# A hybrid attention trunk on one core: two groups of transposes one step later, the second row block's w2 sums in other PSUM banks, the first evacuations in another order

## The chip, the cores and the metric

One core of a Trainium2 chip runs the whole program. The time is device microseconds (us), the median of three runs: 1257.64 us (1256.57 to 1257.86). A difference of about 0.2%, 2.5 us, is what such a measurement can tell from no change.

## What is computed

Two layers, each of a half-step SwiGLU feed-forward, a mixer of three parallel branches, and a second half-step feed-forward, on 256 tokens of width 1024. Cut to what matters here:

```
x = x + 0.5 * (silu(n(x) @ w1) * (n(x) @ w3)) @ w2          # d_ff = 2816
h = n(x);  z = h @ W_in                                     # queries, keys, values, gates of all branches
y_na  = neighbourhood attention;  y_gla = gated linear attention;  y_mla = latent attention
mixed = sig(g0) * (y_na @ w_br_na) + sig(g1) * (y_gla @ w_br_gla) + sig(g2) * (y_mla @ w_br_mla)
x = x + mixed @ w_out
x = x + 0.5 * (second SwiGLU)
```

## The kernel before

All products are made from pairs of fp32r numbers: a high half and the rest, a low half, and three matmuls (high by high, high by low, low by high) for one fp32 product. The weights come as **units** of 128 x 2048 numbers over the SP queue into three raw buffers. ScalarE (ACT) copies the high half (L142), VectorE (DVE) subtracts it from the raw numbers to give the low half (L148), each in two pieces of 128 x 1024. The two L148 of a unit are called a *pair* below. Four buffers hold split units.

Nothing is scheduled by a tool: each engine takes its instructions in the order in which the program is written. Side work stands in small generators (tasks). After each piece of matmuls the program calls `tick()`: it first issues splits for the units ahead (`fill`), and then advances each waiting task whose count has run down. `spawn(gen, n)` sets the first count, `yield n` the next. So one count more puts a task's next step behind one more piece of 12 matmuls (of 128 x 512), and on every engine behind what else that tick issues.

PSUM has eight banks, in two groups of four: `acc` (sums) and `ta` (transposes and attention). A new tile takes the bank of its group that has been free for longest, and its first writer waits for the last reader of that bank.

The places that the change touches:

- **`wide_out`** makes the sums with w2 (11 units) or w_out (4 units) for the row blocks t = 0 and 1, two banks each. For all units but the last two it goes unit by unit, t = 0 and then t = 1, 12 matmuls each; the last two units are held and done at the end, output half by output half. In the feed-forward it follows `fform`, whose 20 chunks (i = 2 to 21) each take two `acc` banks; DVE's L481 is the last to read them.
- **`ffn` at the start of the program** evacuates three chunks at once (`fdrain`): chunks 0 (in `ta` banks) and 1 (in `acc` banks) come ready made from `start_first`, chunk 2 from the first `fform`. An evacuation of chunk 2 starts with two ACT copies (L480), which DVE's L481 waits for.
- **`na_tr`** transposes the queries of neighbourhood attention (L695, spawned at L1122 with a count of 3).
- **`gla_chain`**, linear attention: the last step scales its output on DVE (eight L1103, 128 x 128 each), and after `yield 1` eight transposes (L695) on TensorE (PE), and the high half (ACT L246) and low half (DVE L247) of the result.
- **`branch`** multiplies each branch's output with its weights, in the order na, mla, gla; four pieces of 12 matmuls each (output half h, row block t). They are called na1 to na4, mla1 to mla4 and gla1 to gla4. DVE multiplies each sum by its gate (L1184 for mla and gla). The add into `mixed` (L1186) is done by GpSimd (POOL) for mla and by DVE for gla.
- **`mix_task`**, spawned in each gla piece (L1188) with a count of 2: four PE transposes (L1195) of a finished block of `mixed`, high half on ACT (L246), low half on DVE (L247). The four tasks are called T1 to T4, in the order of gla1 to gla4. T1 and T2 hold output half 0 for t = 0 and 1. The first unit of w_out reads T1 for t = 0 and T2 for t = 1. In each piece of `wide_out` the first four matmuls read the high half, and the fifth is the first to read the low half.

Of the kernel before, what the change touches and what calls it, by code (L numbers as in the profile page):

```python
# [45 lines left out]
def body(tc, T):  # L46
# [3 lines left out]
    with ctx:  # L50
# [146 lines left out]
        def spawn(gen, wait=1):  # L197
            tk = Task(gen, wait)
            tasks.append(tk)
            return tk  # L200
# [181 lines left out]
        def run(g):  # L382
            return spawn(g)
# [30 lines left out]
                    tick()  # L414
            return tks

        def wide_out(first, lhs, nu, done):
            accs = {}
            hold = []
            for u in range(nu):  # L420
                hl = unit()
                if u >= nu - 2:
                    hold.append((u, hl))
                    continue
                for t in range(2):
                    if u == 0:
                        accs[t] = (acc_t(), acc_t())
                    wide_burst(accs[t], lhs, u, hl, t, u == 0, False)
                    tick()
            for t in range(2):  # L430
                for h in range(2):
                    for u, hl in hold:
                        for kk in range(2):
                            a = kk * 1024 + h * 512
                            mm(accs[t][h], lhs(0, u, kk, t), hl[:, 0, a:a + 512], False, False)
                            mm(accs[t][h], lhs(0, u, kk, t), hl[:, 1, a:a + 512], False, False)
                            mm(accs[t][h], lhs(1, u, kk, t), hl[:, 0, a:a + 512], False, u == nu - 1 and kk == 1)
                    done(t, h, accs[t][h])
                    tick(True)
# [12 lines left out]
        def ffn(norms, after, prefetch, first=None, out=None):  # L452
# [42 lines left out]
            def fform(i):  # L495
                hl = unit()
                acc = [(at_t() if first is not None and i == 3 else acc_t()) for _ in range(2)]
                for b in range(2):
                    o = acc[b].rearrange("p (w t n) -> p w t n", w=2, t=2)
                    for k in range(8):  # L500
                        a = k * 256 + b * 128
                        both = xT[:, :, :, k, :].rearrange("p t w n -> p w t n")
                        mm(o, hl[:, 0, a:a + 128], both, k == 0, False)
                        mm(o[:, 0], hl[:, 1, a:a + 128], xT[:, :, 0, k, :], False, k == 7)
                    if b == 0:
                        tick()
                if i == (FIRST_R if first is not None else 2):
                    rs_bcast()
                    if first is not None:
                        for j in range(2):  # L510
                            drains[j] = run(fdrain(j, first[j][0][:, :256], first[j][1][:, :256]))
                        for j, a in held:
                            drains[j] = run(fdrain(j, a))
                if "x" in rs_b:
                    drains[i] = run(fdrain(i, acc))
                else:
                    held.append((i, acc))
                tick()

            us, drains, held = {}, {}, []  # L520
# [33 lines left out]
                if out is None:  # L554
                    after(t, h)

            wide_out(True, lhs, NCH, done)


        def mixer(l, norms, after, prefetch):  # L560
# [444 lines left out]
            def gla_chain(deps):  # L1005
# [94 lines left out]
                for t in range(2):  # L1100
                    for h in range(4):
                        sl = slice(h * 128, h * 128 + 128)
                        DVE.scalar_tensor_tensor(out=gy[t][:, sl], in0=gy[t][:, sl], scalar=rr[t][:, h:h + 1],  # L1103
                                                 in1=sg[t][:, sl], op0=ALU.mult, op1=ALU.mult)
                yield 1
                for j in range(2):
                    ps = four(gy, j * 256)
                    ysplit(ps, "gla", j)
# [10 lines left out]
            u_tk = []  # L1119
            dense8(512, ev_v, between=up_proj(0, 384, ev_uq, u_tk))  # L1120
            nq = dense8(512, ev_nqk("q"))
            q_tk = spawn(na_tr("q", nq), 3)  # L1122
            dense8(512, ev_copy(gvt), between=up_proj(1, 512, ev_ukv, u_tk))
            mla_tk = spawn(mla_chain(u_tk), 1)
            gl_tk = spawn(gla_gates(), 1)
# [42 lines left out]
            def branch(i, key):  # L1168
                lh = lambda hl, k, t: yT[key, k // 2][hl][:, (k % 2) * 256 + t * 128:(k % 2) * 256 + t * 128 + 128]
                for h in range(2):  # L1170
                    hl = unit()
                    for t in range(2):
                        acc = acc_t()
                        burst(acc, lh, hl, range(4), t, 512, True, True)
                        if i < 2:
                            g = gates[:, t, i * 1024 + h * 512:i * 1024 + h * 512 + 512]
                        else:
                            g = late.pop((h, t))
                        if i == 0:
                            m = mixed[h, t] = s2()  # L1180
                            DVE.tensor_tensor(out=m, in0=acc, in1=g, op=ALU.mult)  # L1181
                        else:
                            m = mixed[h, t]
                            DVE.tensor_tensor(out=g, in0=acc, in1=g, op=ALU.mult)  # L1184
                            e = DVE if i == 2 else POOL
                            e.tensor_tensor(out=m, in0=m, in1=g, op=ALU.add)  # L1186
                        if i == 2:
                            mt[h, t] = spawn(mix_task(h, t), 2)  # L1188
                        tick()

            def mix_task(h, t):
# [19 lines left out]
            def done(t, h, acc):  # L1211
                sl = slice(h * 512, h * 512 + 512)
                DVE.tensor_tensor(out=x[:, t, sl], in0=acc, in1=x[:, t, sl], op=ALU.add)
                after(t, h)
            wide_out(True, lhs, 4, done)


        def spawner(ap, into, params_of=None):
# [146 lines left out]
```

## Time and profile before

| | |
|---|---|
| median of three runs | 1257.64 us (1256.57, 1257.64, 1257.86) |
| the profiled execution's own time | 1256.21 us |
| its span, first to last instruction | 1254.4 us |
| PE busy (matmul / weight load) | 1237.7 us (99%) / 1058.5 us (84%) |
| DVE / ACT / POOL busy | 894.8 (71%) / 710.4 (57%) / 219.4 us (17%) |
| DMA | 228.58 MB, mean 182 GB/s |
| chain that ended last | PE 93%, DVE 4%, ACT 1%, DMA 1%, issue 1% |

A view by time gives an instruction's start, its length, engine, line, what it writes and reads, a count where equal ones follow each other, and in brackets how long the engine stood idle before it and what ended that. Ends of matmuls are modelled and overlap the next start by some 0.16 us, so gaps on PE are read from the idle time in brackets or from starts.

### The profile page before, as it was taken

How to read it: one execution, taken by the hardware profiler on the slowest of the kernel's cores; microseconds unless marked ns; L12 is line 12 of the kernel's file. 1: busy time of each engine (PE TensorE's matmuls, PEld its weight loads, DVE VectorE, ACT ScalarE, POOL GpSimd, SP SyncE). 2: the span in 40 equal slices, each digit the busy share in tenths (PEclk: the TensorE clock that was granted, in tenths of full speed). 3: DMA queues.
4: the chain of work that ended last, by engine and by line, in shares of the span. 5: the costliest groups of instructions: out<-in, count | busy, mean ns of one | idle time of the engine just before them, and what ended most of it. 6: DMA issues, size and time to landing. Idle time of an engine off the chain costs nothing.

```text
span 1254.4 us, 18062 instructions
## 1 busy us (share of the span) xinstructions
PE 1237.7 (99%) x6996; PEld 1058.5 (84%) x6996; DVE 894.8 (71%) x1382; ACT 710.4 (57%) x1303; POOL 219.4 (17%) x167
## 2 busy tenths in 40 slices
PE   7999999999999999999999999999999999999998
PEld 7888888889987888888888888888899878888887
DVE  5888736679755868887378886375896577788862
ACT  6556535657665465655366555355686644665541
POOL 0222101132011112221012220021322020122200
PEclk9999999999999999999999999999999999999999
DMA  8655644562543544556345556347526434555560
GB/s 304 214 185 201 234 169 160 175 222 93 197 171 132 198 172 170 200 181 248 142 171 222 184 185 241 128 162 246 175 91 208 166 134 171 199 201 174 196 235 34
DMA packets 37942, 228.58 MB, mean 182 GB/s; under 512 B 5776, under 2 KB 6928, under 8 KB 13280
## 3 DMA queue, kind: packets, MB, share of 16 engines
q1 hardware_dynamic: 37680, 227.36, 51.1%
q8 instruction: 55, 0.90, 0.3%
q14 instruction: 31, 0.25, 0.1%
q0 software_dynamic: 32, 0.07, 0.0%
q10 hardware_dynamic: 144, 0.00, 0.0%
HBM read 224.26 MB, written 1.05 MB: 180 GB/s over the span
## 4 chain that ended last, share of the span: by engine, by line
PE 93%; DVE 4%; ACT 1%; DMA 1%; issue 1%; POOL 0%; DVEq 0%; SPq 0%; ACTq 0%
PE acc L372 86%; PE ta L372 4%; DVE hl L148 2%; PE ta L695 1%; DMA raw<-in_l_f_w 1%; PE ta L263 1%; ACT junk L1095 0%; POOL sm L573 0%; PE ta L782 0%; ACT hl L142 0%; PE ta L1195 0%; PE ta L680 0%; DVE s L489 0%; DVE s L1181 0%; DVE s L1103 0%
## 5 line engine op out<-in xcount | busy, mean ns | idle before, releaser
L148 DVE TENSOR_TENSOR hl<-raw,hl 128x1024 fp32r<-128x1024 f32 (+2 forms) x422 | 568.1, 1386 | 95.4 <-ACT hl L142 84.5
L142 ACT ACTIVATE hl<-raw 128x1024 fp32r<-128x1024 f32 (+2 forms) x422 | 417.1, 1040 | 103.8 <-PE acc L372 89.9
L372 PE MATMUL acc<-xT,hl 128*128 128x512 f32 (+1 forms) x2768 | 472.8, 332 | 0.9 <-DVE s L481 0.5
L372 PEld LDWEIGHTS acc<-xT,hl 128*128 128x128 f32 x2768 | 413.6, 188 | 57.8 <-DVE s L481 0.8
L372 PE MATMUL acc<-hl,xT 128*128 128x512 f32 (+1 forms) x1584 | 361.8, 383 | 0.0
L372 PEld LDWEIGHTS acc<-hl,xT 128*128 128x128 f32 x1584 | 291.8, 188 | 46.9 <-issue 1.7
L372 PE MATMUL acc<-hl,s 128*128 128x512 f32 x1344 | 312.3, 392 | 0.9 <-DVE s L481 0.9
L372 PEld LDWEIGHTS acc<-hl,s 128*128 128x128 f32 x1344 | 252.0, 189 | 54.2 <-DVE s L481 1.3
L482 POOL TENSOR_TENSOR s<-s,rsb 128x512 f32<-128x512 f32 x80 | 111.9, 1399 | 355.8 <-DVE s L481 355.8
L491 ACT ACTIVATE s<-s 128x256 fp32r<-128x256 f32 x82 | 34.2, 418 | 172.5 <-DVE s L489 172.5
L481 DVE TENSOR_TENSOR s<-acc,s 128x256 f32<-128x256 f32 x158 | 59.7, 419 | 58.5 <-ACT s L480 58.5
L573 POOL TENSOR_TENSOR sm<-sm,mhalf 128x4 f32<-128x4 f32 (+2 forms) x24 | 35.8, 1493 | 200.4 <-DVE sm L577 198.9
L284 POOL TENSOR_TENSOR sm<-sm,mhalf 128x1 f32<-128x1 f32 x12 | 14.1, 1176 | 295.1 <-DVE sm L283 295.1
L480 ACT ACTIVATE s<-acc 128x256 f32<-128x256 f32 x158 | 50.6, 371 | 0.0
L266 ACT ACTIVATE xT<-ta,gain 128x128 fp32r<-128x128 f32 x80 | 22.8, 368 | 35.6 <-PE ta L263 35.6
L247 DVE TENSOR_TENSOR s<-ta,s 128x512 fp32r<-128x512 f32 (+1 forms) x46 | 26.7, 604 | 22.6 <-ACT s L246 22.3
L246 ACT ACTIVATE s<-ta 128x512 fp32r<-128x512 f32 (+1 forms) x46 | 23.0, 531 | 34.4 <-PE ta L695 14.7
L487 ACT ACTIVATE s<-s 128x256 f32<-128x256 f32 x82 | 34.2, 419 | 11.2 <-POOL s L482 0.8
L550 DVE SCALAR_TENSOR_TENSOR x<-acc,x 128x512 f32<-128x512 f32 (+1 forms) x20 | 11.3, 580 | 39.7 <-PE acc L372 39.7
L372 PEld LDWEIGHTS ta<-s,s 64*64 64x64 f32 (+3 forms) x720 | 30.6, 145 | 7.0 <-issue 5.9
L372 PE MATMUL ta<-s,s 64*64 64x128 f32 (+4 forms) x720 | 35.9, 260 | 0.0
L493 DVE TENSOR_TENSOR s<-s,s 128x256 fp32r<-128x256 f32 x82 | 34.0, 416 | 1.9 <-ACT s L491 1.9
(161 smaller groups left out, 643.9 us busy)
## 6 DMA issues: line engine op xcount, KB each, us to landing
raw<-in_l_f_w SPq DMA_DIRECT2D x124, 1024.0 KB, 4.8
raw<-in_l_in_g SPq DMA_DIRECT2D x16, 816.0 KB, 4.4
raw<-in_l_in_late SPq DMA_DIRECT2D x8, 1024.0 KB, 4.9
raw<-in_l_out SPq DMA_DIRECT2D x8, 1024.0 KB, 4.8
raw<-in_l_f_up SPq DMA_DIRECT2D x6, 1024.0 KB, 4.8
raw<-in_l_in_m SPq DMA_DIRECT2D x4, 1024.0 KB, 4.7
raw<-in_l_in_gr SPq DMA_DIRECT2D x4, 1024.0 KB, 4.9
raw<-in_l_in_r SPq DMA_DIRECT2D x4, 1024.0 KB, 4.8
```

The costliest lines, as they stand in the source:

```text
L142: ACT.activation(out=hls[j][:, 0, sl], in_=raws[j][:, sl], func=AF.Copy)
L148: DVE.tensor_tensor(out=hl[:, 1, sl], in0=r[:, sl], in1=hl[:, 0, sl].bitcast(F32), op=ALU.subtract)
L246: ACT.activation(out=hi, in_=ps, func=AF.Copy)
L247: DVE.tensor_tensor(out=lo, in0=ps, in1=hi.bitcast(F32), op=ALU.subtract)
L372: PE.matmul(out=out, lhsT=lhsT, rhs=rhs, start=start, stop=stop, skip_group_check=True)
L480: ACT.activation(out=g[:, j, :], in_=a[j][:, 256:], func=AF.Copy)
L481: DVE.tensor_tensor(out=g[:, j, :], in0=a[j][:, :256], in1=g[:, j, :], op=ALU.add)
L482: POOL.tensor_tensor(out=g, in0=g, in1=rb[:, None, :].to_broadcast([128, 2, 256]), op=ALU.mult)
L487: ACT.activation(out=g[:, 0, :], in_=g[:, 0, :], func=AF.Silu)
L491: ACT.activation(out=o[:, 0, :], in_=g[:, 0, :], func=AF.Copy)
L493: DVE.tensor_tensor(out=o[:, 1, :], in0=g[:, 0, :], in1=o[:, 0, :].bitcast(F32), op=ALU.subtract)
L573: POOL.tensor_tensor(out=r[:, :n], in0=ss[:, :n], in1=mhalf[:, :n], op=ALU.pow)
```

## The change

Five edits:

1. `wide_out` is told from which group the banks of t = 1 come: `ta` in the feed-forwards, `acc` as before for w_out.
2. The first evacuations go 1, 2, 0 where they went 0, 1, 2.
3. `gla_chain` yields 2 where it yielded 1 between the scaling and the transposes.
4. The task with the transposed queries is spawned with 4 where it was 3.
5. `mix_task` is spawned with 3 where it was 2.

```diff
-        def wide_out(first, lhs, nu, done):
+        def wide_out(bank1, lhs, nu, done):
...
                     if u == 0:
-                        accs[t] = (acc_t(), acc_t())
+                        accs[t] = (bank1(), bank1()) if t else (acc_t(), acc_t())
...
                     if first is not None:
-                        for j in range(2):
-                            drains[j] = run(fdrain(j, first[j][0][:, :256], first[j][1][:, :256]))
+                        drains[1] = run(fdrain(1, first[1][0][:, :256], first[1][1][:, :256]))
                         for j, a in held:
                             drains[j] = run(fdrain(j, a))
                 if "x" in rs_b:
                     drains[i] = run(fdrain(i, acc))
                 else:
                     held.append((i, acc))
+                if first is not None and i == FIRST_R:
+                    drains[0] = run(fdrain(0, first[0][0][:, :256], first[0][1][:, :256]))
                 tick()
...
-            wide_out(True, lhs, NCH, done)
+            wide_out(at_t, lhs, NCH, done)
...
-                yield 1
+                yield 2
                 for j in range(2):
                     ps = four(gy, j * 256)
                     ysplit(ps, "gla", j)
...
-            q_tk = spawn(na_tr("q", nq), 3)
+            q_tk = spawn(na_tr("q", nq), 4)
...
-                            mt[h, t] = spawn(mix_task(h, t), 2)
+                            mt[h, t] = spawn(mix_task(h, t), 3)
...
-            wide_out(True, lhs, 4, done)
+            wide_out(acc_t, lhs, 4, done)
```

No instruction is added or taken away. Lines of the changed kernel are one higher from L510 on.

DVE in layer 0, from the last scaling of linear attention on (s_3847 and s_3856 are high halves of that branch's transposed output). Before:

```order
L1103 SCALAR_TENSOR_TENSOR s_3702<-s_3702,sm,s_1955 128x128 x4
L1184 TENSOR_TENSOR gates<-acc,gates 128x512
L247 TENSOR_TENSOR s_3848<-ta,s_3847 128x512
L247 TENSOR_TENSOR s_3857<-ta,s_3856 128x512
L1184 TENSOR_TENSOR gates<-acc,gates 128x512
L148 TENSOR_TENSOR hl<-raw,hl 128x1024 x2
L1184 TENSOR_TENSOR gates<-acc,gates 128x512 x2
L148 TENSOR_TENSOR hl<-raw,hl 128x1024 x2
```

The same place on DVE now:

```order
L1104 SCALAR_TENSOR_TENSOR s_3702<-s_3702,sm,s_1955 128x128 x4
L1185 TENSOR_TENSOR gates<-acc,gates 128x512 x2
L148 TENSOR_TENSOR hl<-raw,hl 128x1024 x2
L247 TENSOR_TENSOR s_3867<-ta,s_3866 128x512
L247 TENSOR_TENSOR s_3876<-ta,s_3875 128x512
L1185 TENSOR_TENSOR gates<-acc,gates 128x512 x2
L148 TENSOR_TENSOR hl<-raw,hl 128x1024 x2
```

The two low halves of linear attention's output now stand behind mla2's gate product and behind a pair. The pairs are called C, D, E and F in this order; C and D are the two shown here.

DVE a little later in layer 0, from gla2's add on (s_3717 is the block of T2, s_3792 that of T3, s_3810 that of T4; `xT` is what the transposed blocks are split into). Before:

```order
L1186 TENSOR_TENSOR s_3717<-s_3717,s_3497 128x512
L148 TENSOR_TENSOR hl<-raw,hl 128x1024 x2
L247 TENSOR_TENSOR xT<-ta,xT 128x512
L1184 TENSOR_TENSOR s_3595<-acc,s_3595 128x512
L1186 TENSOR_TENSOR s_3792<-s_3792,s_3595 128x512
L247 TENSOR_TENSOR xT<-ta,xT 128x512
L1184 TENSOR_TENSOR s_3657<-acc,s_3657 128x512
L1186 TENSOR_TENSOR s_3810<-s_3810,s_3657 128x512
L148 TENSOR_TENSOR hl<-raw,hl 128x1024 x2
L247 TENSOR_TENSOR xT<-ta,xT 128x512 x2
```

The same place on DVE now:

```order
L1187 TENSOR_TENSOR s_3717<-s_3717,s_3497 128x512
L148 TENSOR_TENSOR hl<-raw,hl 128x1024 x2
L1185 TENSOR_TENSOR s_3595<-acc,s_3595 128x512
L1187 TENSOR_TENSOR s_3792<-s_3792,s_3595 128x512
L247 TENSOR_TENSOR xT<-ta,xT 128x512
L1185 TENSOR_TENSOR s_3657<-acc,s_3657 128x512
L1187 TENSOR_TENSOR s_3810<-s_3810,s_3657 128x512
L148 TENSOR_TENSOR hl<-raw,hl 128x1024 x2
L247 TENSOR_TENSOR xT<-ta,xT 128x512 x2
```

The low half of T1 now stands behind gla3's product and add, that of T2 behind gla4's product and add and behind a pair (F; the pair in the second row is E). On PE the transposes of T1 to T4 each stand one piece later: T1 behind gla3 where it stood behind gla2, T2 behind gla4, T3 behind the first piece of w_out, T4 behind the second.

PE at the start of the first `wide_out` (s_366 to s_447 are chunks 0 to 3 of the hidden layer). Before:

```order
L372 MATMUL acc<-hl,s_366 128x512 x6
L372 MATMUL acc<-hl,s_369 128x512 x6
L372 MATMUL acc<-hl,s_366 128x512 x6
L372 MATMUL acc<-hl,s_369 128x512 x6
L372 MATMUL acc<-hl,s_395 128x512 x6
```

The same place on PE now:

```order
L372 MATMUL acc<-hl,s_370 128x512 x6
L372 MATMUL acc<-hl,s_366 128x512 x6
L372 MATMUL ta<-hl,s_370 128x512 x6
L372 MATMUL ta<-hl,s_366 128x512 x6
L372 MATMUL acc<-hl,s_394 128x512 x6
```

The third and fourth rows, the first piece of t = 1, now write `ta` banks. In the program these two were last read by the first evacuations of chunk 0.

## Rows read from the trace of the kernel before

**Rows 1.** The page, part 1: busy time, share of the span, instructions.

```profile
PE 1237.7 (99%) x6996; PEld 1058.5 (84%) x6996; DVE 894.8 (71%) x1382; ACT 710.4 (57%) x1303; POOL 219.4 (17%) x167
```

**Rows 2.** PE's longest wait inside the program: for whom, us in total, times, longest.

```profile
PE ta L695 <- DVE s L1103: 4.2, 4, 1.6
```

**Rows 3.** PE by time, end of the mixer in layer 0.

```profile
390.99 8.46 PE L372 MATMUL acc<-hl,s 128*128 128x512 f32 x36
401.07 0.50 PE L695 MATMUL ta<-idt,s 128*128 128x128 f32 x2 [1.63 <-DVE s L1103]
402.03 1.26 PE L695 MATMUL ta<-idt,s 128*128 128x128 f32 x6 [0.46 <-DVE s L1103]
402.95 15.40 PE L372 MATMUL acc<-hl,s 128*128 128x512 f32 x60
418.55 0.63 PE L1195 MATMUL ta<-idt,s 128*128 128x128 f32 x4 [0.20 <-DVE s L1186]
...
428.17 0.60 PE L1195 MATMUL ta<-idt,s 128*128 128x128 f32 x4
428.52 3.68 PE L372 MATMUL acc<-hl,xT 128*128 128x512 f32 x15
```

**Rows 4.** PE by time, the same place in layer 1.

```profile
1023.06 13.90 PE L372 MATMUL acc<-hl,s 128*128 128x512 f32 x60
1037.15 0.63 PE L1195 MATMUL ta<-idt,s 128*128 128x128 f32 x4 [0.20 <-DVE s L1186]
...
1047.14 8.23 PE L372 MATMUL acc<-hl,xT 128*128 128x512 f32 x35
```

**Rows 5.** Stretches: length, busy us (instructions) by engine, granted clock, DMA share, GB/s.

```profile
403.00:406.50 3.50, 3.50 (x10) 2.78 (x10) 1.65 (x3) 2.74 (x4) 1.29 (x1) 0.54 0.52 218
1023.00:1026.50 3.50, 3.50 (x17) 2.90 (x17) 2.12 (x4) 2.83 (x4) 1.30 (x1) 1.00 0.56 232
```

**Rows 6.** PE by time, first feed-forward: one early chunk, then the start of `wide_out`.

```profile
44.69 90.71 PE L372 MATMUL acc<-xT,hl 128*128 128x512 f32 x512 [0.48 <-DVE s L481]
135.24 2.91 PE L372 MATMUL acc<-hl,s 128*128 128x512 f32 x12
139.06 6.27 PE L372 MATMUL acc<-hl,s 128*128 128x512 f32 x26 [0.91 <-DVE s L481]
```

**Rows 7.** DVE by time, the first evacuations: L481 of chunk 2.

```profile
30.97 0.76 DVE L481 TENSOR_TENSOR s<-acc,s 128x256 f32<-128x256 f32 x2 [1.84 <-ACT s L480]
```

**Rows 8.** PE by time, the transposed queries in layer 1.

```profile
889.52 0.63 PE L695 MATMUL ta<-idt,s 128*128 128x128 f32 x4 [0.25 <-DVE s L830]
```

**Rows 9.** DVE by time, end of the mixer in layer 0.

```profile
400.59 2.18 DVE L1103 SCALAR_TENSOR_TENSOR s<-s,sm,s 128x128 f32<-128x128 f32 x8
402.69 0.68 DVE L1184 TENSOR_TENSOR gates<-acc,gates 128x512 f32<-128x512 f32 x1
...
408.11 3.45 DVE L148 TENSOR_TENSOR hl<-raw,hl 128x1024 fp32r<-128x1024 f32 x2
...
413.56 3.44 DVE L148 TENSOR_TENSOR hl<-raw,hl 128x1024 fp32r<-128x1024 f32 x2
416.93 0.68 DVE L1184 TENSOR_TENSOR s<-acc,s 128x512 f32<-128x512 f32 x1
...
418.39 0.69 DVE L1184 TENSOR_TENSOR s<-acc,s 128x512 f32<-128x512 f32 x1
...
419.79 2.35 DVE L148 TENSOR_TENSOR hl<-raw,hl 128x1024 fp32r<-128x1024 f32 x2
422.06 0.68 DVE L247 TENSOR_TENSOR xT<-ta,xT 128x512 fp32r<-128x512 f32 x1
```

**Rows 10.** POOL by time, the same stretch: mla's four adds.

```profile
403.44 1.29 POOL L1186 TENSOR_TENSOR s<-s,gates 128x512 f32<-128x512 f32 x1 [5.15 <-DVE gates L1184]
408.33 2.14 POOL L1186 TENSOR_TENSOR s<-s,gates 128x512 f32<-128x512 f32 x1 [3.60 <-DVE gates L1184]
412.30 3.62 POOL L1186 TENSOR_TENSOR s<-s,gates 128x512 f32<-128x512 f32 x2 [1.83 <-DVE gates L1184]
```

## The prediction

> **What bounds the kernel now.** The page's busy line shows PE at 99% of the span [rows 1], so only what PE waits for, or the clock it is given, can be won. The view of PE's waits has, beside the start of the program, one entry that matters: the transposes of linear attention's output wait for their scaling on DVE, 4.2 us in four pieces, two to a layer [rows 2]. PE by time then says where. In layer 0 the third piece of the mla branch ends at 390.99 + 8.46 = 399.45; the transposes start at 401.07 after 1.63 us idle, stand again for 0.46, and matmuls go on at 402.95 [rows 3]. DVE's eight scalings run from 400.59 to 402.77 [rows 9], so PE goes on as soon as they are done. The next 60 matmuls take 15.40 us there and 13.90 in layer 1 [rows 3, 4]: in the 3.5 us from 403.0 the granted clock averages 0.54, hence largely 1.2 GHz, and 10 matmuls run, where in layer 1, behind the same two waits, it is 1.00 (2.4 GHz) and 17 run [rows 5]. So layer 0 also pays 15.40 - 13.90 = 1.5 us for the clock. The other waits that the edits touch are 0.20 us at T1 in both layers [rows 3, 4], 0.48 and 0.91 in the first feed-forward [rows 6], and 0.25 at the transposed queries in layer 1 [rows 8].
>
> **Other banks for t = 1.** At the first `wide_out` the second piece should start at 135.24 + 2.91 = 138.15 and starts at 139.06, held by DVE's L481 of the last chunk, which has to free its `acc` banks [rows 6]. The `ta` banks have been free since the start, so the 0.91 goes. It can't come back from the hidden layer: the last chunk is needed only by the eleventh unit. The other three feed-forwards show no such wait. At their end two `ta` banks are held, and the third norm transposes must take a bank again that the first used two pieces of matmuls earlier; that reader is a DVE step of four small instructions, so I cost it at nothing. **-0.9** (0 to -1.1).
>
> **Order 1, 2, 0.** Before, DVE finishes chunks 0 and 1, and stands 1.84 us until ACT has copied chunk 2 [rows 7]. Now ACT copies it one activation earlier and chunk 0's two products fill DVE's time behind it. That brings chunk 2 forward by a few tenths and pushes the next weight split back by about as much. What decides is the 0.48 at 44.69, where PE waits for the end of this queue [rows 6]. Ends: nothing, or all 0.48; **-0.3**, since the chunks' last subtracts now fill a gap of DVE between two evacuations.
>
> **Queries one piece later.** The wait for L830 is 0.25 [rows 8]; a piece of 12 matmuls, 13.90 / 5 = 2.78 us [rows 4], covers it. ACT does its copies one piece later, and the next to need one of their banks stands several pieces on. **-0.3**.
>
> **Linear attention and the mixed rows.** I work out layer 0 in the times of rows 3 and 9.
>
> First without new waits. PE does mla2 in the gap: 399.45 + 2.78 = 402.23, before the last scaling (402.77). The transposes then end as before, 402.95, but five other pieces follow, mla3 to gla3: 402.95 + 13.90 (full clock, since the gap is gone) = 416.85 for T1. T1 to T4 are (428.17 - 418.55) / 3 = 3.21 apart [rows 3], so T4 starts at 426.48 and the third piece of w_out at 426.8. Before, the second piece starts at 428.52 and the third 3.21 - 0.35 = 2.86 later, at 431.4. That is **-4.55** in layer 0. In layer 1: 1023.06 + 13.90 + 9.63 + 0.35 = 1046.95, against 1047.14 + 2.86 = 1050.0 [rows 4]: **-3.05**.
>
> Now DVE. It is nearly full here, and the edits put T1's and T2's low halves behind more of its work. How POOL's adds weigh on it can be read off [rows 9, 10]. An add takes 1.29 alone (403.44). The one at 408.33 takes 2.14, as if it had started only when the first copy of a pair that began at 408.11 was done (409.2); the pair takes 3.45 in place of 2.35, as if its second copy had then waited for the add. The next pair shows the same. So adds and copies take turns, each waiting for the whole of the other. In the changed order both gate products stand ahead of C, so two adds wait at a pair's start where one did.
>
> Steps of DVE by starts in rows 9: a gate product 0.6, product and add 418.39 - 416.93 = 1.46, a free pair 422.06 - 419.79 = 2.27, a low half of a block 0.6. From 402.69: two products, 403.9; C waits for the first add (403.44 + 1.29 = 404.73), its copies and the second add alternate: 404.73 + 2.27 + 1.29 = 408.3; two low halves, 409.5 (gla1 starts at 402.95 + 2 x 2.78 = 408.5 and needs the first, done at 408.95, in its third matmul at 408.97: just in time); two products, 410.7; third add from 410.3 to 411.6, D and the fourth add, 415.2 (gla3 starts at 414.1 and needs D's second copy at 415.5); gla1 and gla2, 418.1; E, 420.4; gla3, 421.8; T1's low half done at **422.5**; gla4, 423.9; F, 426.15; T2's low half done at **426.9**.
>
> PE starts the first piece of w_out at 416.85 + 3.21 + 0.35 = 420.41 and reads T1's low half four matmuls (4 x 0.23) later, at 421.34: it waits 1.15. The second piece starts at 424.77 and wants T2's at 425.7: 1.2 more. So 2.35 us a layer come back, and it is **-2.2 and -0.7**. All later pairs and T3, T4 have 5 us and more, because their readers stand in the held part.
>
> The Trainium skill has the rule behind this, in "SBUF — State Buffer", section "Who interferes with whom": a VectorE instruction with two SBUF inputs and a GpSimd instruction that reads SBUF exclude each other, and the later one waits for the whole of the earlier. L148 has two SBUF inputs, and by that rule the sum below is 4.4, where a mere slowdown of pairs would give 8.4 (second case). The trace agrees with the rule (2.14 against 1.29).
>
> **Sum**: 0.9 + 0.3 + 0.3 + 2.2 + 0.7 = 4.4. The profiled execution (1256.21) would take 1251.8. The three runs stand 0.4, 1.4 and 1.65 above it. If the two upper had a second fall of the clock (1.5), in layer 1, that goes too, and the median becomes 1256.21 + 0.4 - 4.4 = 1252.2; if not, 1257.64 - 4.4 = 1253.2. I take **1252.7**.
>
> The Trainium skill's "TensorE: Matmul & The Clock Gate", section "Part 1: The HAM clock gate (the "warmup" mystery)", says that the number of slow matmuls varies from run to run of one kernel. By that rule the 1.5 is there or not by chance, and the sum is 4.4 or 2.9 by what the run compared with had; the trace agrees in so far as two equal gaps had one fall.
>
> **Rivals.**
>
> *The low halves come in time.* If a pair beside adds costs 3.45 whatever waits there, as its rows also allow, C ends at 407.3, D at 413.2, F at 424.2, T2's low half at 424.9 against a need of 424.55, and T1's not late at all. Then 0.35 a layer comes back, the sum is 1.5 + 4.2 + 2.7 = 8.4, and the time 1257.64 - 8.4 = 1249.2. Against it stand the two adds at C's start.
>
> *DVE gives it all back.* If T1 and T2 are later still (an ACT high half behind splits, another turn lost to an add), the whole of 4.55 and 3.05 is gone where the two waits reach that sum, that is with T2's low half at 429.1 in layer 0. What is left is 1.5: 1256.1.
>
> *The clock falls at the new waits: slower than before.* PE stood 1.63 + 0.46 = 2.09 us within 2 us in layer 0 and the clock fell [rows 3, 5]; it would now stand 1.15 and 1.2 within 5 us, twice. Each fall costs 1.5. With a fall at all four, 1252.7 + 6.0 = 1258.7; it decides from the fourth fall on, since three give 1257.2. Against it: in layer 1 the 2.09 cost no clock, and the new gaps are shorter each.
>
> *The wait only moves.* The scalings end at 402.77 whatever PE does, so if DVE ran them later the transposes would wait as before, now with one piece less behind them. Nothing ahead of them changes on DVE, so I give it no more than the rest.
>
> **How the numbers follow.** Forecast 0.54 (1251 to 1254.5, one fall of the clock included), low halves in time 0.24 (1248.3 to 1250.5), all given back 0.15 (1255 to 1257), clock 0.04, the rest 0.03. The range 1248.3 to 1256.5 leaves out under 2 in 10. A measurement can tell 0.2%, 2.5 us: faster than 1255.1 is the forecast, the second case and a little of the third, 0.80; within 2.5 us the third and most of the clock case, 0.17; slower 0.03.
>
> **What would show it.** Right: no wait of L695 for L1103 above 0.7 us; clock 1.00 from 403 to 406; the second piece of the first `wide_out` without idle time; new waits of PE for DVE's L247 at the fifth matmul of the first two w_out pieces, near 1.2 us each; a pair C of some 4.4 us from the moment that its gate products are done, with two adds in it. Wrong: no wait for L247 there (second case), one of over 2 us or a new one at gla1 or gla3 (third), a granted clock near a half at w_out (fourth). If the third chunk from the start still waits about 0.5 at its bank, the new order of evacuations brought nothing.

## The result and the profile after

The changed kernel takes 1249.17 us (median of 6 runs, 1248.38 to 1250.16), the kernel before beside it 1256.31 (6 runs, 1254.61 to 1257.86). The ratio is 0.9943, 95% interval 0.993 to 0.9956: **7.1 us faster**, where 4.4 were forecast from the profiled run and 1252.7 us as the time. By the interval the gain is 5.5 to 8.8 us. The profiled execution after took 1248.38 us, with a span of 1246.6. Lines are one higher than before from L510 on.

The busy line of the page after, as [rows 1]:

```profile
PE 1234.3 (99%) x6996; PEld 1057.1 (85%) x6996; DVE 896.4 (72%) x1382; ACT 709.5 (57%) x1303; POOL 219.7 (18%) x167
```

PE's waits inside the program. Of the entry of [rows 2], 4.2 us for the scalings, nothing is left; in its place stands one for low halves (for whom: us in total, times, longest):

```profile
PE acc L372 <- DVE xT L247: 2.2, 4, 0.8
```

PE by time in layer 0, beside [rows 3]:

```profile
387.94 11.18 PE L372 MATMUL acc<-hl,s 128*128 128x512 f32 x48
398.96 1.13 PE L696 MATMUL ta<-idt,s 128*128 128x128 f32 x8
399.85 13.90 PE L372 MATMUL acc<-hl,s 128*128 128x512 f32 x60
413.59 0.60 PE L1196 MATMUL ta<-idt,s 128*128 128x128 f32 x4
413.94 3.02 PE L372 MATMUL acc<-hl,s 128*128 128x512 f32 x12
416.80 0.60 PE L1196 MATMUL ta<-idt,s 128*128 128x128 f32 x4
417.15 1.17 PE L372 MATMUL acc<-hl,xT 128*128 128x512 f32 x4
418.67 2.11 PE L372 MATMUL acc<-hl,xT 128*128 128x512 f32 x8 [0.34 <-DVE xT L247]
420.62 0.60 PE L1196 MATMUL ta<-idt,s 128*128 128x128 f32 x4
420.98 1.18 PE L372 MATMUL acc<-hl,xT 128*128 128x512 f32 x4
422.94 2.10 PE L372 MATMUL acc<-hl,xT 128*128 128x512 f32 x8 [0.78 <-DVE xT L247]
424.87 0.60 PE L1196 MATMUL ta<-idt,s 128*128 128x128 f32 x4
```

Four pieces (x48: na3, na4, mla1, mla2) now stand ahead of linear attention's transposes, where [rows 3] have three (x36). (The prediction calls the last of those three the third piece of mla; it is mla1, as the prediction's own count of what follows has it, and no number hangs on that.) No row up to the first piece of w_out at 417.15 has a bracket: PE stood nowhere. There it does four matmuls and stops, twice, for the low halves of T1 and of T2. What a stop costs is read from starts, not from the bracket. A piece without a stop takes 416.80 - 413.94 = 2.86 to the next transposes; the first piece of w_out takes 420.62 - 417.15 = 3.47, the second 424.87 - 420.98 = 3.89. So the brackets of 0.34 and 0.78 cost 0.61 and 1.03. Layer 1 has brackets of 0.32 and 0.78.

The same stretch as the first of [rows 5] (length, busy us by engine, granted clock, DMA share, GB/s): the clock is 1.00, 17 matmuls run in it, not 10.

```profile
403.00:406.50 3.50, 3.50 (x17) 2.90 (x16) 3.50 (x4) 1.52 (x2) 0.93 (x1) 1.00 0.12 28
```

PE by time in the first feed-forward, beside [rows 6]. From 31.48 on nothing waits for an evacuation, and the second piece of `wide_out`, now in `ta` banks, starts 2.75 after the first.

```profile
25.75 5.90 PE L372 MATMUL ta<-xT,hl 128*128 128x512 f32 x32
31.48 18.74 PE L372 MATMUL acc<-xT,hl 128*128 128x512 f32 x104
...
133.36 2.91 PE L372 MATMUL acc<-hl,s 128*128 128x512 f32 x12
136.11 2.88 PE L372 MATMUL ta<-hl,s 128*128 128x512 f32 x12
```

DVE by time in layer 0, from the first gate product of mla on, beside [rows 9]:

```profile
399.63 1.28 DVE L1185 TENSOR_TENSOR gates<-acc,gates 128x512 f32<-128x512 f32 x2
400.83 4.18 DVE L148 TENSOR_TENSOR hl<-raw,hl 128x1024 fp32r<-128x1024 f32 x2
404.94 1.27 DVE L247 TENSOR_TENSOR s<-ta,s 128x512 fp32r<-128x512 f32 x2
...
407.33 4.23 DVE L148 TENSOR_TENSOR hl<-raw,hl 128x1024 fp32r<-128x1024 f32 x2
411.48 0.68 DVE L1185 TENSOR_TENSOR s<-acc,s 128x512 f32<-128x512 f32 x1
...
414.26 2.36 DVE L148 TENSOR_TENSOR hl<-raw,hl 128x1024 fp32r<-128x1024 f32 x2
...
417.93 0.68 DVE L247 TENSOR_TENSOR xT<-ta,xT 128x512 fp32r<-128x512 f32 x1
...
419.93 2.35 DVE L148 TENSOR_TENSOR hl<-raw,hl 128x1024 fp32r<-128x1024 f32 x2
422.20 1.28 DVE L247 TENSOR_TENSOR xT<-ta,xT 128x512 fp32r<-128x512 f32 x2
```

And POOL's adds beside pairs C and D, as in [rows 10], now two to a pair:

```profile
400.39 3.54 POOL L1187 TENSOR_TENSOR s<-s,gates 128x512 f32<-128x512 f32 x2 [5.14 <-DVE gates L1185]
406.95 3.52 POOL L1187 TENSOR_TENSOR s<-s,gates 128x512 f32<-128x512 f32 x2 [3.02 <-DVE gates L1185]
```

Taken one by one, the first add ends at 401.69, C's first copy at 402.77, the second add at 403.93 and C's second copy at 405.01: each starts its work only when the other engine is done. Pairs C and D take 4.18 and 4.23, E and F, with no add beside them, 2.36 and 2.35. T1's low half ends at 418.61 and T2's at 422.88, and PE goes on at 418.67 and 422.94.

### The profile page after: what moved, and what is told of

It is laid out like the page before. It is cut to its first block, busy times and chain, and to the rows that moved or that the text cites. A ratio compares the mean times of both kernels' runs of the same rounds, so it can differ in the third digit from the quotient of the medians.

```text
span 1246.6 us, 18067 instructions
## 1 busy us (share of the span) xinstructions
PE 1234.3 (99%) x6996; PEld 1057.1 (85%) x6996; DVE 896.4 (72%) x1382; ACT 709.5 (57%) x1303; POOL 219.7 (18%) x167
## 4 chain that ended last, share of the span: by engine, by line
PE 91%; DVE 6%; ACT 1%; issue 1%; DMA 1%; POOL 0%; DVEq 0%; SPq 0%; ACTq 0%; POOLq 0%
PE acc L372 74%; PE ta L372 14%; DVE hl L148 4%; PE ta L696 1%; PE ta L263 1%; ACT junk L1096 0%; DVE gates L1185 0%; DVE s L1185 0%; DMA s<-in_l_bias 0%; PE ta L783 0%; DVE s L1187 0%; DVE s L1104 0%; DMA gcol<-in_gcol 0%; PE ta L681 0%; DVE s L247 0%
## 5 line engine op out<-in xcount | busy, mean ns | idle before, releaser
L372 PE MATMUL acc<-hl,s 128*128 128x512 f32 x816 | 194.4, 391 | 0.0
L372 PEld LDWEIGHTS acc<-hl,s 128*128 128x128 f32 x816 | 152.4, 188 | 32.2 <-issue 0.7
L372 PE MATMUL ta<-hl,s 128*128 128x512 f32 (+1 forms) x624 | 148.0, 386 | 0.0
L372 PEld LDWEIGHTS ta<-hl,s 128*128 128x128 f32 x624 | 116.2, 188 | 22.5
L481 DVE TENSOR_TENSOR s<-acc,s 128x256 f32<-128x256 f32 x158 | 59.6, 419 | 58.9 <-ACT s L480 58.9
```

The source lines that it names most:

```text
L372: PE.matmul(out=out, lhsT=lhsT, rhs=rhs, start=start, stop=stop, skip_group_check=True)
L481: DVE.tensor_tensor(out=g[:, j, :], in0=a[j][:, :256], in1=g[:, j, :], op=ALU.add)
```

## The experiments

Twelve runs were made: nine new kernels, one of them twice, and the kernel before twice more. Times are medians. Each group of runs had its own runs of the kernel before beside it, but none of the changed kernel, so two new kernels are best compared by starts on PE, or by their ratios. The mean clock of a run is the granted clock over its whole span, 1.000 for 2.4 GHz throughout.

### Which edits carry the gain

**Edits 3 and 5 alone**, on the kernel before:

```diff
-                yield 1
+                yield 2
                 for j in range(2):
                     ps = four(gy, j * 256)
...
-                            mt[h, t] = spawn(mix_task(h, t), 2)
+                            mt[h, t] = spawn(mix_task(h, t), 3)
```

> Edits 3 and 5 alone (linear attention's transposes and those of the mixed rows one step later), everything else as before. Theory A, by the starts of the two profiled runs: the two low halves cost 0.6 and 1.0 us a layer at w_out, so edits 3 and 5 bring 3.1 in layer 0 (1.5 of it the clock) and 1.6 in layer 1: 4.7, the time about 1251.6. Theory B, the sum on record: the low halves cost 2.35 a layer and the edits bring 2.9: about 1253.4. Both: no wait for the scalings, granted clock 1.00 behind them. For the start of the program (rows of before): if the 1.27 us by which the fifth chunk starts sooner in the changed kernel is chance, it shows in some runs with the old order of the first evacuations too; if it belongs to the new order, the chunk starts at 32.7 here.

Measured: 1251.05 us, all six runs between 1250.90 and 1251.44, the kernel before 1256.16 (22 runs, 1253.42 to 1258.84); ratio 0.9957 (0.9943 to 0.9971). That is theory A. Mean clock 1.000 in every run. The two early waits stay, as they should. PE by time, at the seventh chunk (chunks are 32 matmuls each from the fourth on, so the 0.48 of [rows 6] is the seventh's too) and at the start of `wide_out`:

```profile
44.06 2.26 PE L372 MATMUL acc<-xT,hl 128*128 128x512 f32 x11 [0.48 <-DVE s L481]
...
138.46 1.75 PE L372 MATMUL acc<-hl,s 128*128 128x512 f32 x6 [0.94 <-DVE s L481]
```

**Edits 1, 2 and 4 alone**: the changed kernel with edits 3 and 5 undone.

```diff
-                yield 2
+                yield 1
                 for j in range(2):
                     ps = four(gy, j * 256)
...
-                            mt[h, t] = spawn(mix_task(h, t), 3)
+                            mt[h, t] = spawn(mix_task(h, t), 2)
```

> Edits 1, 2 and 4 alone (other banks, order 1, 2, 0, queries one piece later); the mixer's last transposes as before. Theory A: 1.1 for the banks, 0.6 for the order, 0.3 for the queries: 2.0, the time about 1254.3; the start of the fifth chunk scatters by some 1.3 from run to run whatever the order. Rival: the earlier start belongs to the new order, then 3.3 and 1253.0, the fifth chunk near 31.5. The sum on record has 1.5 and 1254.8. Both: the waits of 1.6 and 0.46 for the scalings are there in both layers, and the clock falls behind them in layer 0, in layer 1, in both or in none; each fall costs 1.5.

Measured: 1253.04 (1251.33 to 1254.08, 10 runs); ratio 0.9976 (0.9965 to 0.9987), so 1.6 to 4.4 us. The time is the rival's, but its reason isn't: the fourth chunk started at 26.47 in this profile and at 27.00 in a second one of the same kernel (below), and the fifth follows 5.7 later in all. In the other kernels with the new order it started between 25.57 and 26.60, with the old order at 25.92 (twice), 26.38 and 27.02. So the start scatters by 1.1 to 1.4 us whatever the order. From the fourth chunk to `wide_out` the two profiles here take 107.83 and 107.81, all ten with the new order 107.60 to 107.83, the four with the old order 108.13 to 108.23: the new order is worth 0.3 to 0.6, about the 0.48 of [rows 6]. The two halves of the change add up to 5.1 + 3.1 = 8.2 by the medians, more than the 7.1 of the whole; the intervals (3.6 to 7.2 and 1.6 to 4.4) cover that.

**Edit 3 without edit 5**: the changed kernel with a count of 2 for `mix_task`.

```diff
-                            mt[h, t] = spawn(mix_task(h, t), 3)
+                            mt[h, t] = spawn(mix_task(h, t), 2)
```

> The changed kernel without edit 5: the mixed rows' transposes with a count of 2 again, linear attention's transposes still one step later. Theory A: DVE's work ahead of gla1's add is the same but PE comes one piece (2.78) sooner to T1, so T1 waits about 2.0 us for that add in each layer in place of 0.2, T2 to T4 and the low halves at w_out don't wait: 2.0 lost for 1.65 won back, 1249.2 + 0.7 = 1249.9, and up to 3 more if the clock falls behind the new wait as it did behind the old one. Rival: T1 waits 0.2 as before and the low halves are in time: 2.9 faster than the changed kernel, 1246.3.

Measured: 1252.06 (1249.94 to 1253.18, 7 runs); ratio 0.9963 (0.9949 to 0.9976). PE by time, T1 in layers 0 and 1:

```profile
413.56 0.63 PE L1196 MATMUL ta<-idt,s 128*128 128x128 f32 x4 [2.08 <-DVE s L1187]
...
1030.92 0.63 PE L1196 MATMUL ta<-idt,s 128*128 128x128 f32 x4 [2.05 <-DVE s L1187]
```

Theory A to the tenth: T1 waits 2.08 and 2.05, and w_out has no stop. The profiled run, with a clock of 1.000, took 1249.94, as expected (1249.9). The six others had a mean clock of 0.999 (five) or 0.998 (one) and took 1251.23 to 1253.18. That the clock fell behind the gap of 2.08 in them is likely, but not shown: the profile has no fall, a mean of 0.999 comes without one too (below), and the run at 0.998 is the fastest of the six. Behind the changed kernel's stops of 0.34 and 0.78 its profile has no fall.

**Edit 5 without edit 3**: the changed kernel with `yield 1` in `gla_chain`.

```diff
-                yield 2
+                yield 1
                 for j in range(2):
                     ps = four(gy, j * 256)
```

> The changed kernel without edit 3: linear attention's transposes where they were, the mixed rows' still one step later. Both theories: the waits of 1.6 and 0.46 for the scalings are back in both layers. Theory A: T1 then waits no longer (0.2 less a layer), the low half of T2 comes some 1 us late at the second piece of w_out where the clock did not fall, and in time where it did; so the time is that of the kernel before less the early edits' 2.0 and within 1.5 of that: 1254.3 (1253 to 1256). Rival: most of the gain is edit 5's, then 1251 or less.

Measured: 1252.46 (1250.85 to 1256.58, 12 runs); ratio 0.9972 (0.9961 to 0.9984). That is 1.8 less than I expected, but 0.6 from edits 1, 2 and 4 alone, which are also 1.3 under their own expectation. The waits of 1.63 and 0.46 are back in both layers, and no low half has a bracket at w_out (the second piece, from 425.10 to 428.10, is 0.14 longer than a free one). So edit 5 alone brings little: the stretch of layer 1 in the table further down takes 49.46 here and 49.72 before. Edit 3 needs edit 5, or its gap moves to T1.

### Where the clock falls

**Edits 1, 2 and 4 alone, a second profile** (the kernel of the second run above).

> Edits 1, 2 and 4 alone once more, for one look at where the clock falls: theory, behind the wait for the scalings in layer 0, in layer 1 or both, 1.5 us each; rival, elsewhere in the program too.

Measured: 1252.39, clock 0.999, and no fall in either layer: the 60 matmuls behind the waits take 13.89 and 13.87. PE by time in layer 0:

```profile
401.04 13.89 PE L372 MATMUL acc<-hl,s 128*128 128x512 f32 x60
```

The first profile of the same kernel had there

```profile
400.46 15.43 PE L372 MATMUL acc<-hl,s 128*128 128x512 f32 x60
```

Same kernel, same waits (1.63 and 0.46): the fall comes in one run and not in another. The 0.999 is of the end of the program: the clock is 1.00 up to the last matmul, and averages 0.58 in the last 1.6 us, where PE has nothing left to do.

**The kernel before, two more profiles** (lines are one higher here, by a comment at the top).

> The kernel before, one more look: theory, the granted clock falls behind the wait for the scalings in layer 0, in layer 1, in both or in neither, and nowhere else; each fall makes the 60 matmuls behind it 15.4 us in place of 13.9. The start of the fourth chunk lies between 25.5 and 27.1.

> The kernel before, a third look, with the same expectation as the second.

The first took 1253.65. PE by time:

```profile
25.92 5.90 PE L373 MATMUL ta<-xT,hl 128*128 128x512 f32 x32
...
134.05 2.89 PE L373 MATMUL acc<-hl,s 128*128 128x512 f32 x12
138.02 4.26 PE L373 MATMUL acc<-hl,s 128*128 128x512 f32 x17 [1.08 <-DVE s L482]
...
390.02 8.45 PE L373 MATMUL acc<-hl,s 128*128 128x512 f32 x36
...
401.93 13.87 PE L373 MATMUL acc<-hl,s 128*128 128x512 f32 x60
...
439.73 0.60 PE L264 MATMUL ta<-idt,x 128*128 128x128 f32 x4
```

The second took 1255.34. Its row for the same 60 matmuls:

```profile
401.99 15.50 PE L373 MATMUL acc<-hl,s 128*128 128x512 f32 x60
```

The clock in the stretch of [rows 5], in the first:

```profile
403.00:406.50 3.50, 3.50 (x17) 2.91 (x16) 2.14 (x4) 3.24 (x4) 1.47 (x2) 1.00 0.25 105
```

and in the second:

```profile
403.00:406.50 3.50, 3.50 (x11) 2.76 (x10) 0.67 (x2) 1.76 (x2) 0.83 (x1) 0.59 0.27 112
```

The two profiles differ by 1.69 us in time and by 15.50 - 13.87 = 1.63 in this row. So the first is the kernel before with no fall, and what [rows 3, 5] showed is one fall. Of the six profiles that keep the gap, four fell in layer 0 (15.40, 15.43 and 15.50 for 60 matmuls, and with edit 5 but not edit 3 17.86 for 72, where layer 1 has 16.60). None fell in layer 1, or elsewhere ahead of the last matmul. The 42 timed runs of the kernel before, by mean granted clock of the run:

| mean clock | runs | us |
|---|---|---|
| 1.000 | 4 | 1253.4 to 1254.0 |
| 0.999 | 8 | 1253.5 to 1257.1 |
| 0.998 | 17 | 1254.9 to 1257.1 |
| 0.997 | 13 | 1256.9 to 1258.8 |

A mean of 1.000 leaves no room for a fall, but 0.999 does not tell one fall (the profile of [rows 3]) from a low clock at the end of the program alone (the profile at 1252.39). One fall and such an end gave 0.998 in three profiles.

**The gap filled.** Edits 1, 2 and 4 alone, and in front of linear attention's transposes:

```diff
                 yield 1
+                pad = tr_t()
+                for i in range(9):
+                    mm(pad, xT[:, 0, 0, 0, :], xT[:, 0, 0, 4:8, :].rearrange("p k n -> p (k n)"), i == 0, i == 8)
```

> Edits 1, 2 and 4 alone, and in front of linear attention's transposes nine more matmuls of 128 x 512 (2.04 us) into a bank that nobody reads, so that PE works where it stood for 2.09 us. Theory (the scatter of the kernel before is the clock, which falls behind this gap or not): the granted clock is 1.000 in every run, the runs lie within some 0.6 us of each other, and the time is that of the undisturbed runs of edits 1, 2 and 4 alone, 1251.3 to 1251.7, with the wait still paid in full. Rival (the scatter has another source): it stays at 1253.0, spread over 2 us or more.

Measured: 1252.31 (1251.17 to 1253.79, 7 runs); ratio 0.9967 (0.9956 to 0.9978). PE by time, the nine matmuls and what is left of the wait:

```profile
396.26 2.21 PE L372 MATMUL ta<-xT 128*128 128x512 f32 x9
...
399.02 1.12 PE L696 MATMUL ta<-idt,s 128*128 128x128 f32 x6 [0.33 <-DVE s L1104]
```

Half of the theory holds: with PE at work in the gap the mean clock is 1.000 in all seven runs. The other half falls: the runs still lie 2.6 us apart, and the median is 0.6 above the upper end of what I expected. It is 0.7 below that of edits 1, 2 and 4 alone, which the intervals do not separate. So the clock is not the only source of scatter. The start of the program is another (up to 1.5 us by the fourth chunk, between profiles). Whether it is all of the rest, these runs can't tell, since only one run of this kernel has a trace.

### What makes the low halves late

**T2's low half ahead of pair F**: behind the gla pieces the tasks go ahead of the splits.

```diff
                             mt[h, t] = spawn(mix_task(h, t), 3)
-                        tick()
+                        tick(i == 2)
```

> The changed kernel, but behind the four gla pieces the waiting tasks go ahead of the splits; on DVE that changes one thing, T2's low half now stands ahead of pair F. Theory A (the wait at the second piece of w_out is F's): the idle 0.78 there goes, and by starts 1.0 us a layer; the 0.35 at the first piece stays: 2.0 faster than the changed kernel, about 1247.2. Rival (DVE's low half is late whatever stands ahead of it, or F late in its place makes PE wait for L148): no gain, 1249.2 or above.

Measured: 1248.01 (1246.16 to 1249.16, 5 runs); ratio 0.9932 (0.9919 to 0.9944). The profiled run took 1246.16. The stop at the second piece is gone in both layers, that at the first piece stays (PE by time, layer 0):

```profile
418.56 2.13 PE L372 MATMUL acc<-hl,xT 128*128 128x512 f32 x8 [0.34 <-DVE xT L247]
```

By the medians it is 1.2 faster than the changed kernel where 2.0 were expected; the intervals of the two overlap. By the trace theory A holds: the stretch from na3 to the norm's transposes takes 47.28 and 47.26 in the two layers, against 48.29, so 2.0 in both.

**Half of pair E behind T1's low half as well**:

```diff
-        def tick(fill_last=False):
+        def tick(fill_last=False, skip=False):
...
-            if fill_last:
+            if fill_last and not skip:
                 fill()
...
-                        tick()
+                        tick(i == 2, (h, t) == (0, 1))
```

> As the run before in this list, and in addition the splits behind gla2 are left out and made up one piece later, so that half of pair E stands behind T1's low half. Theory A: T1's low half is done 1.1 us sooner and the wait at the first piece of w_out goes too: 1.0 and 0.6 by starts a layer, 3.3 in both, about 1245.9, and PE waits for nothing but the program's start. Rival: the delayed pair makes PE wait for its second half at gla4 or at w_out, and the time stays at 1247 or above.

Measured: **1245.45** (1244.74 to 1246.10, 4 runs); ratio 0.9913 (0.9899 to 0.9926): 10.9 us faster than the kernel before, 3.7 than the changed one, and the fastest of the kernels that leave nothing out. PE's list of waits has one entry of any size left, the program's start:

```profile
PE ta L372 <- ACT hl L341: 6.0, 1, 6.0
```

DVE by time, layer 0:

```profile
414.12 1.22 DVE L148 TENSOR_TENSOR hl<-raw,hl 128x1024 fp32r<-128x1024 f32 x1
...
416.66 0.68 DVE L247 TENSOR_TENSOR xT<-ta,xT 128x512 fp32r<-128x512 f32 x1
417.26 1.22 DVE L148 TENSOR_TENSOR hl<-raw,hl 128x1024 fp32r<-128x1024 f32 x1
...
419.79 0.68 DVE L247 TENSOR_TENSOR xT<-ta,xT 128x512 fp32r<-128x512 f32 x1
420.39 2.35 DVE L148 TENSOR_TENSOR hl<-raw,hl 128x1024 fp32r<-128x1024 f32 x2
```

T1's low half starts at 416.66 and T2's at 419.79, against 417.93 and 422.20 in the changed kernel. The delayed splits hold nobody up.

**Without mla's four adds on POOL**:

```diff
-                            e.tensor_tensor(out=m, in0=m, in1=g, op=ALU.add)
+                            if i == 2:
+                                e.tensor_tensor(out=m, in0=m, in1=g, op=ALU.add)
```

> The changed kernel without mla's four adds on POOL (the mla branch is left out of the mixed rows; all matmuls, products and splits stay). Theory A (adds and pairs take turns, so two adds lengthen pairs C and D from 2.35 to 4.2): C and D take 2.35, the low halves of T1 and T2 come 3 us sooner, PE waits for neither, and the time is 3.3 less than the changed kernel's: 1245.9. Rival (C and D are long for another reason, as a wait for their ACT halves): C and D stay at 4.2, the waits of 0.34 and 0.78 stay, 1249.2.

Measured: 1245.31 (1244.92 to 1246.57, 4 runs); ratio 0.9915 (0.99 to 0.9931). DVE by time, pairs C and D and T1's low half:

```profile
400.60 2.35 DVE L148 TENSOR_TENSOR hl<-raw,hl 128x1024 fp32r<-128x1024 f32 x2
...
406.00 2.35 DVE L148 TENSOR_TENSOR hl<-raw,hl 128x1024 fp32r<-128x1024 f32 x2
...
415.77 0.68 DVE L247 TENSOR_TENSOR xT<-ta,xT 128x512 fp32r<-128x512 f32 x1
```

C and D fall from 4.2 to 2.35, nothing else in the program is taken away, and both stops are gone. Counted from the first gate product of mla, T1's low half starts after 16.37 (415.77 - 399.40) in place of 18.30: 1.9 sooner and not the 3 that I expected, since DVE now stands 0.65 and 1.15 for PE's sums on the way.

**The four adds on DVE**:

```diff
-                            e = DVE if i == 2 else POOL
+                            e = DVE
```

> The changed kernel with mla's four adds on DVE in place of POOL. Theory A: each add costs DVE 0.7, and C and D fall from 4.2 to 2.35 each: 4 x 0.7 - 2 x 1.85 = -0.9, so DVE is 0.8 to 0.9 ahead at T1's low half; the wait at the first piece of w_out (0.6 by starts) goes and of the second 0.2 is left of 1.0: 1.4 a layer, 2.8, the time 1246.4. Rival (POOL's adds don't hold DVE up): DVE is 2.8 later, both waits grow to over 3 us together a layer and the time is 1253 or more.

Measured: 1246.67 (1245.89 to 1247.01, 5 runs); ratio 0.9922 (0.9909 to 0.9934). DVE does four adds more a layer (0.69 each) and is still ahead, since C and D are back at 2.35. C:

```profile
403.12 2.35 DVE L148 TENSOR_TENSOR hl<-raw,hl 128x1024 fp32r<-128x1024 f32 x2
```

PE's stop at the first piece of w_out is gone; at the second a bracket is left that costs 0.6 by starts, where I expected 0.2:

```profile
422.70 2.11 PE L372 MATMUL acc<-hl,xT 128*128 128x512 f32 x8 [0.33 <-DVE xT L247]
```

By starts, na3 to the norm's transposes takes 47.22 in both layers in place of 48.29: 2.1 us in all are won against the changed kernel. By the medians it is 2.5, but the intervals of the two ratios just overlap.

## Why the prediction came out as it did

The direction, the places and the mechanisms were right, and the gain was mis-sized: 4.4 forecast, 7.1 measured. The time lies outside the forecast's own 1251 to 1254.5, and inside the range only by the part of it that the second case brought. That case gave 1249.2, almost the measured time, but by luck, not by its mechanism: the low halves are **not** in time, the stops that it denies are there, and C takes 4.18, not 3.45. Term by term, by starts of rows on PE, between the first further profile of the kernel before (no fall of the clock, 1253.65) and the profile after (1248.38). The mixer's stretch of layer 0, as an example, ends at the first L264 or L263 behind the mixed rows: 439.73 - 390.02 before, and after 436.23 - 387.94 by this row:

```profile
436.23 0.60 PE L263 MATMUL ta<-idt,x 128*128 128x128 f32 x4
```

| stretch | before | after | gain | forecast |
|---|---|---|---|---|
| up to the fourth chunk | 25.92 | 25.75 | 0.17 | 0 |
| to `wide_out` (order 1, 2, 0) | 108.13 | 107.61 | 0.52 | 0.3 |
| its first piece (banks) | 3.97 | 2.75 | 1.22 | 0.9 |
| the stretches with the queries, both layers | 820.87 | 820.34 | 0.53 | 0.3 |
| layer 0, na3 to the norm's transposes in w_out | 49.71 | 48.29 | 1.42 | 0.7 |
| the same in layer 1 | 49.72 | 48.29 | 1.43 | 0.7 |

The sum is 5.3, which is the whole difference of the two runs (5.27), against 4.4 - 1.5 = 2.9 without the clock. So nothing of size is lost elsewhere, at the third norm transposes either, which the prediction cost at nothing. The table rests on one profile of each kernel.

**Mis-sized: the new waits.** This is 1.4 of the 2.4. The step that failed is the sum of DVE's turns, which put T1's low half at 422.5 and T2's at 426.9, hence 1.15 + 1.2 = 2.35 a layer; measured are 0.61 + 1.03 = 1.64. Counted from the first gate product of mla (402.69 in the sum, 399.63 measured), C was to be done after 5.6 and was after 5.3; D after 12.5, was after 11.85; T1's low half after 19.8, was after 19.0; T2's after 24.2, was after 23.25. So C and D carry 0.66 of the 0.96. I had added the printed lengths of adds and copies, 1.29 and 1.13 a turn. In a chain of turns each is shorter: behind the first add come a copy of 1.08, an add of 1.16 and a copy of 1.08, by the ends given above. Two adds and the copy between them take 3.54 (POOL at 400.39), where the sum had 3.71.

**Right: the turns themselves.** C was forecast at 4.4 with two adds in it and took 4.18. With the adds gone, or on DVE, C takes 2.35. So the adds made DVE late and the low halves with it, as far as the rows show by no other way than the pairs. The Trainium skill's rule in "SBUF — State Buffer", section "Who interferes with whom" (a VectorE instruction with two SBUF inputs and a GpSimd one that reads SBUF exclude each other for the whole instruction), agrees with these traces: 4.18 with two adds beside the pair, 2.35 with none.

**Right: scalings, clock, banks, order.** No wait of the transposes for the scalings, a clock of 1.00 behind them, the second piece of `wide_out` 2.75 behind the first, the seventh chunk without its 0.48. The two pieces of `wide_out` start 2.73 to 2.79 apart in all ten profiles with the new banks, 3.82 to 3.97 in the four with the old. The small terms were all a little low. For the banks I took the bracket for the price, 0.91 where it is 1.07 by starts (3.82 - 2.75); of the order's 0.48 I counted 0.3.

**Mis-sized: the clock.** I counted one fall, 1.5 us, because the profiled run had one. Its price was near (1.63 by the row, 1.69 by the time, between the two further profiles). But the price of a median is not that of one profile. The median of the kernel before, 1256.31, stands 2.66 above its profile without a fall, and that of the changed kernel 0.79 above its profile. The difference, 1.87, joined to the 5.3 makes the 7.1. That this is the clock for its larger part is argued, not shown run by run: the runs before have mean clocks down to 0.997 and go with them from 1253.4 to 1258.8, while edits 3 and 5 alone, which take the gap away, lie within 0.54 at 1.000. It is not shown where a second fall comes from: the runs at 0.997 stand lower than the 0.998 and 0.999 of the profiles with one fall, and no profile has two. The Trainium skill's "TensorE: Matmul & The Clock Gate", section "Part 1: The HAM clock gate (the "warmup" mystery)", says, of a kernel's start, that the number of slow matmuls varies from run to run. The traces show the same in the middle of a kernel: the same one with the same waits took 15.43 and 13.89 for the 60 matmuls.

**The profiled runs were not of one kind.** The run of before that I summed against (1256.21) had a fall and a start that came 1.1 late (27.02 against 25.92); the profile after (1248.38) had neither. Their difference of 7.8 is therefore no measure of the edits; the 5.3, between two profiles without a fall, is nearer to one.

**The rivals.** "DVE gives it all back" fell, since T1's and T2's low halves came earlier than summed, not later. "The clock falls at the new waits" fell for stops of 0.34 and 0.78 (no fall in the profile after, nor in that of edits 3 and 5 alone); for the 2.08 of edit 3 without edit 5 it stays open. "The wait only moves" fell as it was put: the scalings start 9.6 behind the start of na3 in both profiles (400.59 - 390.99, 397.53 - 387.94). But edit 3 without edit 5 does move a wait, to T1 (2.08); edit 5 is what prevents it.

## What to carry to other kernels

Sum a stop by the starts of the work around it, and set one run's profile against another's only when it is known what both lost to the start and to the clock; a gap that costs the clock by chance is worth more in the median than its idle time, if it is taken away (edits 3 and 5 won 5.1 us by the medians and 2.8 by starts; filling the gap with idle work won 0.7, which the intervals don't separate from nothing). When a step is moved behind other work of a nearly full engine, list that work to the end: here the remedy was another order of two splits and two low halves on DVE, worth as much again as half of the change. Two engines whose instructions take turns should not meet at the same place: here it paid to give the idle engine's adds to the full one (2.1 us by starts).

## What was not expected of the hardware

- Four adds more on DVE made DVE earlier: 4 x 0.69 = 2.8 us more work a layer, but C and D 2.35 each in place of 4.18 and 4.23, and 2.1 us less in all by starts on PE (2.5 by the medians, 1249.17 to 1246.67).
- Behind a gap of 1.63 and 0.46 us the clock fell in four of six profiles in layer 0, and in none of the six behind the same gap in layer 1. Two stops of 0.34 and 0.78, 4.3 us apart, had no fall behind them in either layer (the changed kernel, and edits 3 and 5 alone).
- With the clock at 1.000 in all runs a kernel still scattered over 2.6 us (1251.17 to 1253.79), while another lay within 0.54. The start of the program can make up to 1.5 of it (the fourth chunk began between 25.57 and 27.02 in the fourteen profiles of all kernels). The rest is open.
